# Two INNER feed-forward down projections regrouped into sevens over five blocks each

## The chip, the cores and the metric

The program runs on one core of one Trainium2 chip. Its engines work side by side: TensorE (PE) multiplies matrices, VectorE (DVE), ScalarE (ACT) and GpSimd (POOL) compute element by element, and SyncE (SP) issues transfers (DMA), as POOL also does. Each engine works through its own instructions in program order and waits on semaphores for the others. The metric is the device time of one execution in microseconds (us); lower is better.

## The reference

The kernel computes two layers of a decoder on x of 512 tokens by 1024 features, all in fp32. Each layer is a feed-forward network (FFN), a mix of attention and convolution, and a second FFN:

```
def rms_norm(x, gain):
    inv = lax.rsqrt(jnp.mean(x * x, axis=-1, keepdims=True) + NORM_EPS)
    return (x * inv) * gain

def swiglu(h, w_gate, w_up, w_down):
    return (jax.nn.silu(h @ w_gate) * (h @ w_up)) @ w_down

for l in range(2):
    x = x + 0.5 * swiglu(rms_norm(x, ffn1_norm[l]), ffn1_wg[l], ffn1_wu[l], ffn1_wd[l])
    h = rms_norm(x, mix_norm[l])
    z = h @ w_in[l]                      # q, k, v and three convolution streams
    attn_out = sliding_window_attention(q, k, v, attn_sink[l])
    conv_out = short_conv(b_gate, c_gate, h_conv, conv_w[l])
    x = x + jnp.concatenate([attn_out, conv_out], axis=-1) @ w_out[l]
    x = x + 0.5 * swiglu(rms_norm(x, ffn2_norm[l]), ffn2_wg[l], ffn2_wu[l], ffn2_wd[l])
return rms_norm(x, final_norm)
```

The FFN's inner width is 2816. The change touches the product with `w_down` in two of the four FFNs.

## The kernel before

**Products.** An fp32 product is made of three matmuls. Every operand is kept as a high part (`wh`, or the first of a pair) and a low part (`wl`, what the cast to the high part lost), and hi x hi, lo x hi and hi x lo are added up in PSUM. A weight tile of 128 partitions by 1024 values (two row blocks of 128 by 512 columns) is loaded by SP into a buffer `raw` (`load`, L205), cast by ACT into `wh` (L221) and subtracted by DVE into `wl` (L222). There are eight `raw` buffers (`stock`) and four each of `wh` and `wl`. The input side of a product, a "form", is made in the same way: `fb11`, `fb21`, `fb22`, `ft1` to `ft4`.

**Blocks and sevens.** The inner width is cut into 11 blocks of 256. A table per FFN lists its stages. `FIRST` is the first FFN of layer 0, `INNER` the second FFN of layer 0 and the first of layer 1, `LAST` the last. A stage "w" computes gate and up for two blocks, "p" one block plainly. "s" is the down projection of four blocks by the Strassen-Winograd scheme: instead of eight products of quarter matrices it makes seven, from sums of quarters. "d" is the plain down projection of the blocks listed. INNER does the blocks 1 to 4 and 5 to 8 by sevens and 9 and 10 plainly, by `down_end`.

**Sums of weights.** The seven products of an "s" need five weight quarters or sums: a11, s1 (two quarters), a12, s3 (two quarters) and a22, each as two `raw` tiles (halves h = 0 and 1). The sums with two quarters come from a load by SP and an accumulating transfer by POOL onto the same tile (L216). The further sums are made on the chip: s2 = a11 + s1 by DVE in place in a11's tile (L249), s4 = a12 + s2 by a POOL transfer that adds one `raw` tile onto another (`raw<-raw`, L277). A buffer is free for a later load when its last reader, which may be such a transfer, is done. The order of the products is a11, a12, s2, s3, s1, a22, s4 (`FORMS`); in the program of before PE writes them to accumulators x, w, x, y, x, y, x. `share` walks through them and calls `stream` for each weight tile: 12 matmuls of 128x512. After a product, DVE adds the accumulator to x (L1005).

**Activations on their way.** A "w" stage leaves its gated values in planes of 16-bit halves (`pl`, ACT L1227), which SP transposes by DMA (`send`, L1233, into `pt`) and ACT copies into `raw_a` (`join`, L1287). The pair of blocks that is computed last before the sevens is 9 and 10; its accumulators are worked on while the first group of sevens runs.

**What sets the order.** The program is written as one sequence. `need_raw` issues loads a number of units ahead (`LOAD_AHEAD`), `need_split` makes casts and subtractions ahead of use (`SPLIT_AHEAD`), and `tc.issue_after(x)` puts an instruction behind another in the order; a scheduler then places the rest. On an engine, and on SP's and POOL's queues, the order is fixed: what is behind a waiting instruction waits too. In `send` the transposes of a pair stand behind the latest weight load that had been issued.

One form per group, `fb22`, is made "far": ACT writes its negative into the low part and casts the high part, and a POOL transfer adds the original to the low part (`split_far`, L227 to L229), so that DVE has no part in it.

Of the kernel before, what the change touches and what calls it, by code (L numbers as in the profile page):

```python
# [16 lines left out]
P = 128  # L17
# [17 lines left out]
    ("s", 2), ("d", (10,)), ("s", 6),  # L35
)
INNER = (
    ("p", 0), ("w", 1), ("d", (0,)), ("w", 3), ("w", 5), ("w", 7), ("w", 9), ("s", 1), ("s", 5),
    ("d", (9, 10)),
)  # L40
LAST = INNER[:-1] + (("d", (9, 10)),)
# [28 lines left out]
    ((1, 1, -1), (0, 1, 1)), ((0, 1, 1),),  # L70
)
# [4 lines left out]
def trunk_kernel(  # L76
# [130 lines left out]
    def need_raw(u):  # L207

        while state["raw"] <= min(u, len(units) - 1):
            n = state["raw"]  # L210
            _, _, kc, _, wide = units[n][0]
            r = stock(f"raw_{n}", shape=(P, kc, wide * (2 if n in beside else 1)))
            if n >= OPEN:
                load(r, n, 0, kc)
            for more in () if n in beside else units[n][1:]:
                nc.gpsimd.dma_start(out=r, in_=rows_of(*more), accum_op=ALU.add)  # L216
            raw_of[n] = r
            state["raw"] += 1
# [12 lines left out]
    def need_split(g):  # L231
        while state["split"] <= min(g, len(order) - 1):
# [3 lines left out]
            if what in (None, "wide", "room", "far"):  # L236
                need_raw(u if far else u + LOAD_AHEAD)
                raw = raw_of.pop(u)
            elif isinstance(what, tuple):

                what, h, how = what
                far = how == "far"
# [21 lines left out]
            if what == "room":  # L264
                hi, lo = both(f"wx_{n}", shape=(P, 2, 2, S))
            else:
                hi = wpool.tile(shape, F32R, tag="wh", bufs=4, name=f"wh_{n}")
                lo = wpool.tile(shape, F32R, tag="wl", bufs=4, name=f"wl_{n}")
# [4 lines left out]
            if isinstance(order[n][1], tuple):  # L273
# [13 lines left out]
                for i in done:  # L287
                    del raw_of[u + 2 * i + h]
            split_of[n] = (hi, lo)
            state["split"] += 1  # L290
            if far:

                with tc.issue_after(sent.ins):
                    need_raw(u + LOAD_AHEAD + (4 + h if isinstance(order[n][1], tuple) else 0))
# [110 lines left out]
    def down_end(acts, blocks, norm, open_):  # L405

        a, b = blocks
        held = []

        def tile_of(n):  # L410
            while len(held) <= n:
                held.append(take_split(min(SPLIT_AHEAD, 4 - len(held)))[1:])
            return held[n]

        def products(acc, t, n):
            tok = slice(t * P, (t + 1) * P)
            fresh = (t, n // 2) not in open_
            ah, al = acts[blocks[n % 2]]
            wh, wl = tile_of(n)
            for k in range(2):  # L420
                for i, (x_, w) in enumerate(((ah, wh), (al, wh), (ah, wl))):
                    nc.tensor.matmul(
                        acc,
                        x_[:, k, tok],
                        w[:, k, :],
                        start=n % 2 + k + i == 0 and fresh,
                        stop=n % 2 == 1 and k == 1 and i == 2,
                        skip_group_check=not fresh,
                    )

        def bank(t, o):
            if (t, o) in open_:
                return open_[t, o]
            return psum("mm", [P, S], f"down_{state['group']}_{t}_{o}")

        by_hand()
        for t in range(2):
            for o in range(2):
                acc = bank(t, o)
                for i in range(2):  # L440
                    products(acc, t, 2 * o + i)
                yield t, o, acc
        ahead = state["group"]
        for o in range(2):
            accs = {t: bank(t, o) for t in (2, 3)}
            for i in range(2):
                n = 2 * o + i
                for t in (2, 3):
                    products(accs[t], t, n)
                    if i:  # L450
                        yield t, o, accs[t]
                if n in (1, 2):
                    norm.pull()
                if n:
                    need_split(ahead + n)

    def plan():
# [15 lines left out]
        def seven(at, how):  # L473


            u = len(units)
            for what in (((0, 0),), ((1, 0), (1, 1)), ((0, 1),), ((1, 0), (0, 0)), ((1, 1),)):
                for h in range(2):
                    add_unit(*(at(o, j, h) for o, j in what))
            forms = EARLY if how == "early" else FORMS  # L480
            order.extend((u, (what, h, how)) for what in forms for h in range(2))

        def ffn(wg, wu, wd, stages):
            for what, b in stages:
# [13 lines left out]
                if what == "s":  # L498
                    seven(
                        lambda o, j, h: (wd, 2 * b + KC // 2 * j + 2 * h, 2, o * S, S),  # L500
                        "early" if (what, b) == stages[-1] else "share",
                    )
# [3 lines left out]
                for half in range(2):  # L506
                    for k in b:
                        u = add_unit((wd, 2 * k, 2, half * S, S))
                        if half == 0 or not end or stages is not LAST:
                            room = end and stages is not LAST and (half, k) == (0, b[0])  # L510
                            order.append((u, "room" if room else "wide"))
# [227 lines left out]
    class Seven:  # L739
# [3 lines left out]
        def __init__(self, full, room, name, far=()):  # L743
            self.full, self.room, self.name, self.forms, self.sums = full, room, name, {}, None
            self.far = far

        def make(self, *names):
            for what in names:
                if what in self.forms:
                    continue  # L750
                hi, lo = both(f"f{what}_{self.name}")
                self.forms[what] = (hi, lo)
                b11, b12, b21, b22 = (
                    self.full[j][:, :, t * H : (t + 1) * H] for j in range(2) for t in range(2)
                )
                if what in ("t2", "t3") and not self.sums:
                    self.sums = self.room(self.name)
                    nc.vector.tensor_sub(self.sums[0], b12, b22)
                if what == "t2":
                    nc.vector.tensor_sub(self.sums[1], self.sums[0], b11)  # L760
                if what == "t1":
                    nc.vector.tensor_sub(b12, b11, b12)
                if what == "t4":
                    nc.vector.tensor_add(self.sums[1], self.sums[1], b21)
                src = {"b11": b11, "b21": b21, "b22": b22, "t1": b12}.get(what)
                if src is None:
                    src = self.sums[0 if what == "t3" else 1]
                (split_far if what in self.far else split)(hi, lo, src)

# [185 lines left out]
    def stream(accs, wh, wl, xh, xl, h, start, norm=None):  # L955

        for u in range(2):
            tok = slice(u * P, (u + 1) * P)
            for k in range(2):
                for i, (x_, w) in enumerate(((xh, wh), (xl, wh), (xh, wl))):  # L960
                    nc.tensor.matmul(  # L961
                        accs[u],
                        x_[:, 2 * h + k, tok],
                        w[:, k, :],
                        start=start and h + k + i == 0,
                        stop=h + k == 2 and i == 2,
# [5 lines left out]
    def share(  # L972
# [6 lines left out]
        for step, (acc, operand, start) in enumerate(chains):  # L979
# [3 lines left out]
            xh, xl = ops.forms[operand]  # L983
# [5 lines left out]
            for h in range(2):  # L989
# [824 lines left out]
```

## Time and profile before

| | us |
|---|---|
| runs | 1638.86, 1637.8, 1638.81 (median 1638.81) |
| profiled execution | 1635.43 |
| its span on the core | 1633.7 |
| PE busy | 1624.8 (99%) |
| DVE busy | 1304.0 (80%) |
| ACT busy | 1142.0 (70%) |
| first INNER sevens and plain down, PE | 721.20 to 820.90 |
| second INNER sevens and plain down, PE | 1045.90 to 1146.00 |

In the profile's rows, names stand without their buffer numbers (`wl<-raw,wh` is any such subtraction), L numbers are lines of the kernel before, SPq and POOLq are the queues from which transfers are issued, and "to landing" is the time from issue until the data has arrived. A row of waits gives the engine and line that waited, what it waited for, the total, the number of times and the longest. A row of an engine in order of time gives the start, the duration, the instruction and, in brackets, how long the engine had been idle before it and what ended that.

### The profile page before, as it was taken

What the parts mean: (1) busy time and instruction counts of PE and PEld (TensorE: products, weight loads), DVE (VectorE), ACT (ScalarE), POOL (GpSimd) and SP (SyncE); (2) the same over time, 40 slices, a digit from 0 to 9 for tenths busy, and PEclk for the clock granted to TensorE, in tenths of its full rate; (3) what the DMA queues carried; (4) which work ended last, traced back from release to release, by engine and by line L of the source; (5) the groups of instructions that cost most, each with busy time, mean ns of one, the idle gap of its engine ahead of it and who ended that gap; (6) DMA issues with size and microseconds to landing.
All of it is one profiled execution on the core that took longest, in us unless ns stands there. A gap on an engine that the chain in (4) does not pass through costs nothing.

```text
span 1633.7 us, 21063 instructions
## 1 busy us (share of the span) xinstructions
PE 1624.8 (99%) x7544; PEld 1353.7 (83%) x7544; DVE 1304.0 (80%) x1718; ACT 1142.0 (70%) x1597; POOL 192.1 (12%) x172
## 2 busy tenths in 40 slices
PE   9999999999999999999999999999999999999998
PEld 7888888898888888888888888888988888888886
DVE  7987779878899867789688667887678987778885
ACT  7457777558867677786476777865597775777864
POOL 0011111100120111112001111110002101111111
PEclk9999999999999999999999999999999999999999
DMA  9379999934685788999737888997147857899992
GB/s 258 88 196 220 222 224 251 219 90 88 177 200 129 206 207 218 210 235 254 217 82 202 211 211 220 234 246 199 45 108 196 202 132 196 215 213 234 222 248 84
DMA packets 295292, 310.74 MB, mean 190 GB/s; under 512 B 116980, under 2 KB 179476, under 8 KB 295188
## 3 DMA queue, kind: packets, MB, share of 16 engines
q1 hardware_dynamic: 252660, 230.09, 48.7%
q0 software_dynamic: 41824, 78.65, 28.3%
q8 instruction: 59, 0.97, 0.2%
q10 hardware_dynamic: 704, 0.66, 0.1%
q14 instruction: 45, 0.37, 0.1%
HBM read 263.74 MB, written 2.10 MB: 163 GB/s over the span
## 4 chain that ended last, share of the span: by engine, by line
PE 93%; ACT 5%; DVE 1%; DMA 1%; issue 1%; SPq 0%; ACTq 0%; DVEq 0%
PE x L961 25%; PE y L961 13%; PE x_s L961 10%; PE w L961 6%; PE y_s L961 5%; PE up L1118 4%; PE down L383 3%; PE w_s L961 3%; PE acc L313 3%; PE acc L314 3%; PE acc L316 2%; PE acc L360 2%; PE x_m L961 1%; PE xt L705 1%; PE y_m L961 1%; ACT p L1589 1%
## 5 line engine op out<-in xcount | busy, mean ns | idle before, releaser
L222 DVE TENSOR_TENSOR wl<-raw,wh 128x1024 fp32r<-128x1024 f32 (+1 forms) x493 | 599.2, 1221 | 211.3 <-ACT wh L221 204.8
L221 ACT CAST wh<-raw 128x1024 fp32r<-128x1024 f32 (+1 forms) x493 | 511.7, 1044 | 300.3 <-PE y L961 37.5
L961 PE MATMUL x<-wh,ft 128*128 128x512 f32 x608 | 187.2, 389 | 0.0
L961 PE MATMUL y<-wh,ft 128*128 128x512 f32 x608 | 187.1, 389 | 0.0
L961 PE MATMUL x<-wh,fb 128*128 128x512 f32 x608 | 187.1, 389 | 0.0
L961 PEld LDWEIGHTS x<-wh,ft 128*128 128x128 f32 x608 | 114.2, 188 | 23.7
L961 PEld LDWEIGHTS x<-wh,fb 128*128 128x128 f32 x608 | 114.2, 188 | 23.7
L961 PEld LDWEIGHTS y<-wh,ft 128*128 128x128 f32 x608 | 114.1, 188 | 23.7
L961 PE MATMUL x<-wl,fb 128*128 128x512 f32 x304 | 118.3, 389 | 0.0
L961 PE MATMUL x<-wl,ft 128*128 128x512 f32 x304 | 118.3, 389 | 0.0
L961 PE MATMUL y<-wl,ft 128*128 128x512 f32 x304 | 118.3, 389 | 0.0
L1287 ACT COPY raw_a<-pt 128x1024 uint16<-128x1024 uint16 x76 | 103.3, 1360 | 17.9 <-DMA pt<-pl 17.8
L216 POOL DMA_DIRECT2D raw<-in_ffn_wu_dram x39 | 47.0, 1208 | 546.3 <-DMA raw<-in_ffn_wu_dram 351.4
L313 PE MATMUL acc<-hh,wh 128*128 128x512 f32 x240 | 94.0, 392 | 0.0
L961 PE MATMUL w<-wh,fb 128*128 128x512 f32 x304 | 93.6, 389 | 0.0
L314 PE MATMUL acc<-hl,wh 128*128 128x512 f32 x240 | 93.5, 390 | 0.0
L316 PE MATMUL acc<-hh,wl 128*128 128x512 f32 x240 | 93.4, 389 | 0.0
L961 PE MATMUL y_s<-wh,ft_s 128*128 128x512 f32 x256 | 78.8, 389 | 0.0
L961 PE MATMUL x_s<-wh,ft_s 128*128 128x512 f32 x256 | 78.8, 389 | 0.0
L249 DVE TENSOR_TENSOR raw<-raw,raw 128x1024 f32<-128x1024 f32 x58 | 70.5, 1219 | 9.1 <-DMA raw<-in_ffn_wd_dram 6.0
L216 POOL DMA_DIRECT2D raw<-in_ffn_wg_dram x39 | 46.8, 1206 | 235.2 <-DMA raw<-in_ffn_wu_dram 88.4
L961 PE MATMUL x_s<-wh,fb_s 128*128 128x512 f32 x240 | 74.0, 389 | 0.2 <-DVE x L1005 0.2
(370 smaller groups left out, 3431.7 us busy)
## 6 DMA issues: line engine op xcount, KB each, us to landing
raw<-in_ffn_wu_dram SPq DMA_DIRECT2D x120, 512.0 KB, 5.1
raw<-in_ffn_wd_dram SPq DMA_DIRECT2D x104, 512.0 KB, 6.9
raw<-in_ffn_wg_dram SPq DMA_DIRECT2D x80, 512.0 KB, 5.4
raw<-in_ffn_wu_dram POOLq DMA_DIRECT2D x39, 512.0 KB, 8.4
raw<-in_ffn_wg_dram POOLq DMA_DIRECT2D x39, 512.0 KB, 5.9
raw<-in_w_in_dram SPq DMA_DIRECT2D x36, 512.0 KB, 4.5
raw<-in_ffn_wd_dram POOLq DMA_DIRECT2D x32, 512.0 KB, 8.6
raw<-raw POOLq DMA_DIRECT2D x20, 512.0 KB, 8.9
```

The source lines that it names most:

```text
L216: nc.gpsimd.dma_start(out=r, in_=rows_of(*more), accum_op=ALU.add)
L221: cast = nc.scalar.copy(hi, raw)
L222: state["sub"] = eng.tensor_sub(lo, raw, f32(hi))
L249: nc.vector.tensor_add(a11, a11, s1)
L313: nc.tensor.matmul(acc, hi[:, k, :], rhs[k][0], start=k == first, stop=False)
L314: nc.tensor.matmul(acc, hi[:, k, :], rhs[k][1], start=False, stop=False)
L316: state["product"] = nc.tensor.matmul(acc, lo[:, k, :], rhs[k][0], start=False, stop=k == last)
L360: nc.tensor.matmul(accs[j][:, t * H : (t + 1) * H], w[:, k, :], x_, start=t + k + i == 0, stop=k == KC - 1 and i == 2, skip_group_check=True,)
L383: nc.tensor.matmul(acc, a[:, k, tok], w[:, k, :], start=i + k + n == 0 and fresh[t], stop=i == last and k == 1 and n == 2, skip_group_chec ...
L961: nc.tensor.matmul(accs[u], x_[:, 2 * h + k, tok], w[:, k, :], start=start and h + k + i == 0, stop=h + k == 2 and i == 2, skip_group_chec ...
L1118: nc.tensor.matmul(accs[t], x_[:, tok], w[:, k, :], start=j + k + i == 0, stop=j == 3 and k == 1 and i == 2,)
L1287: nc.scalar.copy(room.rearrange("p c (n z) -> p c z n", z=2)[:, :, z, :], turned[0][:, NT * z + 2 * c : NT * z + 2 * c + 2, :],)
```

## The change

INNER's blocks 1 to 10 are now done by two groups of seven products over five blocks each: the first group takes blocks 1 to 4 and, as a fifth, block 5; the second takes 7 to 10 and block 6. The fifth block is split into quarters of half the height: its two row blocks of 128 play the parts of the two halves of the group's inner dimension. So each of the seven products gets, beside its two full weight tiles (128x1024), a third of half the size (128x512, h = 2), and each form gets an extra form of 128x256 (`fx...`, with `sx` for its sums). The plain down projection of blocks 9 and 10 and `down_end` are gone. The half weight tiles and extra forms lie in a pool of 11 smaller buffers (`g2`) that also holds other small tiles.

The order in which the 15 `raw` tiles of a group are loaded is given by `THREES` (or `THREES_EARLY` for the last group of a stage): the number of each tile of a11, s1, a12, s3 and a22. In `THREES`, s1's half tile is loaded as number 7 and s3's as number 13, behind the full tiles of a22 (11 and 12). Loads are issued two units further ahead (`LOAD_AHEAD + 2`). The transposes of the last pair are ordered behind the load that was the latest at step 5 of its products (`seen`), and not behind the latest when they are written; its copies into `raw_a` come from tick 12 on. In the INNER groups the forms `fb11` and `ft1` are made far, as `fb22`. FIRST and LAST keep sevens of four blocks, in another notation.

```diff
 INNER = (
-    ("p", 0), ("w", 1), ("d", (0,)), ("w", 3), ("w", 5), ("w", 7), ("w", 9), ("s", 1), ("s", 5),
-    ("d", (9, 10)),
+    ("p", 0), ("w", 1), ("d", (0,)), ("w", 3), ("w", 5), ("w", 7), ("w", 9), ("s", (1, 3, 5)),
+    ("s", (7, 9, 6)),
 )
-LAST = INNER[:-1] + (("d", (9, 10)),)
+LAST = INNER[:-2] + (("s", (1, 3, None)), ("s", (5, 7, None)), ("d", (9, 10)))
...
+PAIRS = ((0, 1), (2, 3), (4, 5), (6, 7), (8, 9))
+THREES = ((0, 1, 2), (3, 4, 7), (5, 6, 9), (8, 10, 13), (11, 12, 14))
+THREES_EARLY = ((0, 1, 2), (3, 4, 10), (5, 6, 8), (7, 9, 11), (12, 13, 14))
+EXTRA = (("b21+",), ("t1", "t2+"), ("b22", "t4", "t3+"), ("t1+", "t4+"), ("b22+",), (), ())
...
-            r = stock(f"raw_{n}", shape=(P, kc, wide * (2 if n in beside else 1)))
+            room = g2 if kc == 1 else stock
+            r = room(f"raw_{n}", shape=(P, kc, wide * (2 if n in beside else 1)))
             if n >= OPEN:
-                load(r, n, 0, kc)
+                with behind(state["load"] if kc == 1 else None):
+                    load(r, n, 0, kc)
...
-                last = {"a11": 0, "a12": 4, "s2": 2, "s3": 6, "s1": 2, "a22": 8, "s4": 4}[what]
-                need_raw(u + h if far else u + max(last, 4) + h + LOAD_AHEAD)
-                a11, s1, a12, s3, a22 = (raw_of.get(u + 2 * i + h) for i in range(5))
+                last = {"a11": 0, "a12": 2, "s2": 1, "s3": 3, "s1": 1, "a22": 4, "s4": 2}[what]
+                if at is PAIRS:
+                    need_raw(u + max(at[last][h], at[2][h]) + LOAD_AHEAD)
+                else:
+                    need_raw(u + at[last][h] + LOAD_AHEAD + 2)
+                a11, s1, a12, s3, a22 = (raw_of.get(u + at[i][h]) for i in range(5))
...
-            for k in range(2):
+            for k in range(wide):
                 for i, (x_, w) in enumerate(((xh, wh), (xl, wh), (xh, wl))):
...
-                with tc.issue_after(state["load"].ins):
+                with tc.issue_after((seen[0] if wide else state["load"]).ins):
                     nc.sync.dma_start_transpose(
...
+                if step == 5:
+                    seen.append(state["load"])
...
-            plan += [(6 + 2 * gap + gap * n, join, n) for n in range(4)]
+            plan += [(start + gap * n, join, n) for n in range(4)]
...
-            return Seven([raw_act(b), raw_act(b + 2)], room_form, f"s_{whole}_{b}", far=("b22",))
+            far = ("b22",) if x_ is None else ("b11", "t1", "b22")
+            return Seven(full, room_form, f"s_{whole}_{lo}", far=far, extra=extra)
```

Three places in the program, all at the first INNER sevens (layer 0); the second INNER FFN has the same order with other numbers. Here names carry their buffer's number, and the line numbers of the rows marked as after are those of the changed kernel.

SP's queue as PE passes from the last "w" pair to the sevens, before. raw_167 and raw_168 (loaded just ahead) are a12, raw_169 and raw_170 are s3's first load, raw_171 and raw_172 are a22, the DMA_TRANSPOSE rows are the last pair's:

```order
L205 DMA raw_169_6323<-in_ffn2_wd_dram 128x2x512
L205 DMA raw_170_6326<-in_ffn2_wd_dram 128x2x512
L609 DMA gain_3_0_6993<-in_ffn1_norm_dram 128x512
L609 DMA gain_3_1_6994<-in_ffn1_norm_dram 128x512
L205 DMA raw_171_6329<-in_ffn2_wd_dram 128x2x512
L205 DMA raw_172_6363<-in_ffn2_wd_dram 128x2x512
L1233 DMA_TRANSPOSE pt_1_9_6430<-pl_1_9_0_6349 128x8x128
L1233 DMA_TRANSPOSE pt_1_9_6430<-pl_1_9_1_6354 128x8x128
L1233 DMA_TRANSPOSE pt_1_9_6430<-pl_1_9_2_6400 128x8x128
L205 DMA raw_173_6472<-in_ffn2_wd_dram 128x2x512
```

The same place after. raw_171 and raw_173 are s3's full tiles, raw_170 s1's half tile, raw_172 a12's, raw_174 and raw_175 a22's full tiles, raw_176 s3's half tile:

```order
L212 DMA raw_171_6380<-in_ffn2_wd_dram 128x2x512
L212 DMA raw_173_6419<-in_ffn2_wd_dram 128x2x512
L1224 DMA_TRANSPOSE pt_1_9_6440<-pl_1_9_0_6344 128x8x128
L212 DMA raw_170_6361<-in_ffn2_wd_dram 128x512
L1224 DMA_TRANSPOSE pt_1_9_6440<-pl_1_9_1_6349 128x8x128
L1224 DMA_TRANSPOSE pt_1_9_6440<-pl_1_9_2_6402 128x8x128
L212 DMA raw_172_6417<-in_ffn2_wd_dram 128x512
L1224 DMA_TRANSPOSE pt_1_9_6440<-pl_1_9_3_6408 128x8x128
L212 DMA raw_174_6422<-in_ffn2_wd_dram 128x2x512
L212 DMA raw_175_6442<-in_ffn2_wd_dram 128x2x512
L212 DMA raw_176_6461<-in_ffn2_wd_dram 128x512
```

The transposes now stand ahead of a22's two full tiles; s1's half tile stands behind the first transpose, and s3's half tile behind a22's full tiles. raw_174 and raw_175 take the buffers of raw_163 and raw_164 (a11), which are free once the transfers raw_168<-raw_163 and raw_169<-raw_164 have landed.

POOL's queue there, after:

```order
L225 DMA raw_173_6419<-in_ffn2_wd_dram 128x2x512
L225 DMA raw_170_6361<-in_ffn2_wd_dram 128x512
L238 DMA ft1_s_1_1_6532<-raw_a_1_1_5325 128x4x256
L285 DMA raw_168_6322<-raw_163_6149 128x1024
L285 DMA raw_169_6324<-raw_164_6175 128x1024
L238 DMA fb22_s_1_1_6600<-raw_a_1_3_5635 128x4x256
L285 DMA raw_172_6417<-raw_165_6232 128x512
L238 DMA fb11_s_1_7_6716<-raw_a_1_7_6254 128x4x256
L225 DMA raw_176_6461<-in_ffn2_wd_dram 128x512
```

Before, the tile-to-tile transfers were followed by `fb22`'s alone and then by accumulations of the next group; now a half tile's accumulation stands ahead of them and three far forms, a half tile-to-tile transfer and another half tile's accumulation among and behind them.

DVE's order at the second product, a12 (wl_216 to wl_218), after:

```order
L231 TENSOR_TENSOR wl_216_6425<-raw_168_6322,wh_216_6424 128x1024
L1269 TENSOR_TENSOR p7_1_9_1_6252<-p7_1_9_1_6252,gate_1_9_3_6405 128x512
L260 TENSOR_TENSOR raw_165_6232<-raw_165_6232,raw_170_6361 128x512
L231 TENSOR_TENSOR wl_217_6445<-raw_169_6324,wh_217_6444 128x1024
L992 SCALAR_TENSOR_TENSOR x0_89<-x_s_1_1_0_6415,x0_89 128x512
```

The sum onto raw_165 (s2's half tile) stands directly ahead of wl_217, which it had no counterpart for before; the transfer raw_169<-raw_164 waits for wl_217, because it overwrites the tile that wl_217 reads.

DVE's order at the fourth product, s3, after, where wl_224 is its half tile and fxt3 its extra form:

```order
L231 TENSOR_TENSOR wl_224_6588<-raw_176_6461,wh_224_6587 128x512
L747 TENSOR_TENSOR sx_s_1_1_6538<-sx_s_1_1_6538,raw_a_1_5_5945 128x256
L992 SCALAR_TENSOR_TENSOR x2_91<-x_s_1_1_0_6415,x2_91 128x512
L992 SCALAR_TENSOR_TENSOR x2_91<-x_s_1_1_1_6416,x2_91 128x512
L231 TENSOR_TENSOR wl_225_6614<-raw_166_6260,wh_225_6613 128x1024
L231 TENSOR_TENSOR fxt3_s_1_1_6608<-sx_s_1_1_6538,fxt3_s_1_1_6608 128x256
```

Four operations stand between wl_224 and fxt3; PE's matmuls of this half tile need both, and ACT's casts for them in the same order.

More of the change, by code (lines that the diff above doesn't have):

```diff
@@ L509, in ffn @@
                         if half == 0 or not end or stages is not LAST:
-                            room = end and stages is not LAST and (half, k) == (0, b[0])
-                            order.append((u, "room" if room else "wide"))
+                            order.append((u, "wide"))
         for l in range(DEPTH):
@@ L1212, in winograd2 @@
             then = stages[at + 1][0]
+            wide = then == "s" and stages[at + 1][1][2] is not None
+            seen = []
             def apart(t):
```

183 lines of the change are left out of this document (87 added, 96 removed).

## The prediction

> **What bounds the kernel now.** I read the totals and the chain first, then TensorE's waits, then the stage that the change rewrites. From the page:
>
> ```profile
> PE 1624.8 (99%) x7544; PEld 1353.7 (83%) x7544; DVE 1304.0 (80%) x1718; ACT 1142.0 (70%) x1597; POOL 192.1 (12%) x172
> PE 93%; ACT 5%; DVE 1%; DMA 1%; issue 1%; SPq 0%; ACTq 0%; DVEq 0%
> ```
>
> TensorE (PE) is busy 99% of the span and is 93% of the chain that ended last. All that it ever waits for in the trace:
>
> ```profile
> PE idle L150 <- DVE warm L805: 1.2, 1, 1.2
> PE xt L824 <- DMA x<-in_x_dram: 0.3, 1, 0.3
> PE x_s L961 <- DVE x L1005: 0.2, 1, 0.2
> PE y_m L961 <- ACT wh L221: 0.2, 1, 0.2
> ```
>
> Under 2 us in the whole program. So fewer matmuls shorten the span by their own time, and each new wait of PE lengthens it by its own length. Nothing else counts. Now the chain and the stretches (busy time and count of each engine, granted clock, DMA share, GB/s) at the first INNER down projection by sevens, which begins on PE at 721.20; the last row is the second one, in layer 1:
>
> ```profile
> 721.20 5.44 PE x_s L961 x24
> ...
> 737.52 5.44 PE y_s L961 x24
> ...
> 721.20:759.30 38.10, 38.10 (x169) 31.55 (x169) 34.14 (x37) 29.20 (x33) 7.40 (x8) 1.00 1.03 251
> 759.30:797.40 38.10, 38.10 (x169) 31.54 (x169) 33.36 (x34) 22.33 (x23) 4.92 (x5) 1.00 1.03 263
> 721.20:820.90 99.70, 99.70 (x449) 82.73 (x449) 80.91 (x92) 63.83 (x79) 14.72 (x14) 1.00 0.91 225
> 1045.90:1146.00 100.10, 99.91 (x450) 82.61 (x449) 82.45 (x94) 62.46 (x78) 13.28 (x12) 1.00 0.88 216
> ```
>
> 24 matmuls of 128x512 take 5.44 us, 0.2267 each at full clock. PE has no gap, but the DMA share is 1.03 (a share of packet time, so queued packets can carry it past one): in this stage transfers are the tight resource, and the change alters them.
>
> **The change, part by part.** *Matmuls.* Before, an INNER FFN's blocks 1 to 10 take 28 weight tiles of 12 matmuls (two groups of seven products, two tiles each) and 4 plain ones of 24: 432. After, two groups with 14 full tiles of 12 and 7 half tiles of 6 each: 420. So 12 matmuls fewer: 12 x 0.2267 = 2.72 us per FFN, 5.44 in all. FIRST, LAST and the mix stages keep their instructions. This is the only gain on PE.
>
> *The order of loads.* Each half tile brings its own load, and for sums of two weight tiles an accumulating POOL transfer. What such things take, and how they stand in the queues today (SP's waits from 705 to 745, then SP, POOL and ACT in order of time):
>
> ```profile
> SPq L205 <- DMA raw<-raw: 14.1, 2, 11.9
> ...
> 732.78 2.92 SPq L205 DMA_DIRECT2D raw<-in_ffn_wd_dram  x2
> 735.76 7.39 SPq L1233 DMA_TRANSPOSE pt<-pl  x3
> 743.81 1.24 SPq L1233 DMA_TRANSPOSE pt<-pl  x1
> ...
> 720.25 2.41 POOL L216 DMA_DIRECT2D raw<-in_ffn_wd_dram  x2 [10.00 <-DVE wl L222]
> 723.05 0.89 POOL L277 DMA_DIRECT2D raw<-raw  x1 [0.39 <-ACT wh L221]
> ...
> 719.25 2.17 ACT L1227 COPY pl<-u 128x512 uint16<-128x512 uint16 x4
> ```
>
> The loads at 732.78 stood 11.9 us for an accumulation between weight tiles to land and free a buffer, and the transposes behind them in SP's order went out at 735.76, though their first source planes were copied from 719.25 on. The change moves the first transpose ahead of such loads, which costs SP (7.39 + 1.24) / 4 = 2.16 us ahead of whatever follows it. Landings, issue to data (min/median/max), of the SP weight loads and POOL accumulations from 705 to 760, of tile-to-tile accumulations, and of a 256 KB load:
>
> ```profile
> L205 SPq DMA_DIRECT2D raw<-in_ffn_wd_dram x13: 367/419/1017, 707.2 to 752.1; - x13
> ...
> DMA to landing us min/median/max: 4.2/7.7/9.6
> ...
> L216 POOL DMA_DIRECT2D raw<-in_ffn_wd_dram x7: 1188/1197/1231, 707.7 to 758.8; - x7
> ...
> DMA to landing us min/median/max: 7.5/8.7/10.4
> ...
> L277 POOL DMA_DIRECT2D raw<-raw x4: 861/874/886, 723.1 to 766.5; - x4
> ...
> DMA to landing us min/median/max: 8.1/8.9/9.7
> ...
> gain<-in_ffn_norm_dram SPq DMA_DIRECT2D x2, 256.0 KB, 4.2
> ...
> q0 software_dynamic: 835, 2.10, 67.3%
> ```
>
> The last row is POOL's queue from 719 to 736: 2.10 MB used 67.3% of 16 engines for 17 us, 5.45 us per MB. And the vector work in the chains below:
>
> ```profile
> L222 DVE TENSOR_TENSOR wl<-raw,wh 128x1024 fp32r<-128x1024 f32 x43 | 52.3, 1220 | 8.5 <-ACT wh L221 8.3
> ...
> L1005 DVE SCALAR_TENSOR_TENSOR x<-x_s,x 128x512 f32<-128x512 f32 x14 | 9.1, 683 | 0.0
> ...
> L1227 ACT COPY pl<-p 128x512 uint16<-128x512 uint16 x8 | 4.6, 617 | 1.1 <-DVE p L1276 1.1
> ```
>
> PE's own timetable: a product now has two full tiles and a half one, 30 matmuls, 6.80 us. Starting at 721.20, the second product's second tile (wl_217) begins at 730.72 and its low part is wanted at 731.2; the fourth product's half tile (raw_176, wl_224) begins at 747.0, with the low part of its operand fxt3 wanted at 747.3.
>
> *First wait, at wl_217.* On DVE this subtraction stands behind the sum raw_165 += raw_170, so behind raw_170's load and accumulation, and raw_170's load now stands on SP behind the first transpose. Two of the four plane copies are done at about 720.3; transpose 2.16, so 722.5; a 256 KB load, 4.2, so 726.7; POOL starts 0.4 later (0.39 in its row). The trace has no 256 KB accumulation. Bounds: half of the shortest 512 KB one, 3.75, and the median whole, 8.7. I take 6.25, the shortest less its bytes' share (0.25 MB x 5.45 = 1.4, rounded to 1.25), because fixed latency dominates rows of 7.5 to 10.4. So 733.35; the sum 0.69 (as a 128x512 operation), wl_217 1.22: 735.3. PE wants it at 731.2: **a wait of 4.1**, with ends 1.6 and 8.
>
> *Second wait, at wl_224.* raw_169 += raw_164 on POOL is released by wl_217: 735.3 + 0.4, landing 8.9 later, 744.6. Only then is raw_164's buffer free for raw_175, and SP issues raw_176 behind raw_175: 745.0. Load 4.2, POOL 0.4, accumulation 6.25: 755.85. Then wh_224's cast (0.62) and, in DVE's order ahead of what PE needs, wl_224 (0.69), a 128x256 sum (0.42, from the line through 1.22 and 0.69), two additions to x (1.28), wl_225 (1.22) and fxt3 (0.42): 760.5. PE, late by 4.1, arrives at 751.4: **a wait of 9.1**. Without the first wait both sides move together and it stays 9.1. Ends: 5.8 with accumulations of 3.75 and 8.1, and 14 with the load at 7.7 and the others at 8.7 and 9.7. What is late next: the sums behind these loads keep their distance to PE, since PE has slipped by 13 us in front of them.
>
> *More far forms* (a form whose low part is made by an ACT copy and an accumulating POOL transfer instead of a DVE subtraction): three per group where there was one. The one of before makes PE wait nowhere in the rows above. The new ones are made a product ahead, 6.80 us, against a landing of 7 to 9: 0 to 2 us each group. I take 0, as the one of before hid.
>
> *The stage's end.* The two plain blocks, after which the next norm followed, give way to a final group of seven that the norm follows directly. FIRST already ends so, and the list of PE's waits has nothing for it: 0, with 0 to 1 as bounds. DVE's 56 and ACT's 52 more instructions, mostly half and quarter size, are beside PE: DVE was at 34.14 of 38.10 us, so it has about 4 us left per such stretch. The gain vectors' loads, now later on SP, are not wanted before that end.
>
> *Sum per FFN:* -2.72 + 4.1 + 9.1 = +10.5; two of them, **+21.0**. The profiled execution took 1635.43 us (span 1633.7 and 1.7 around it), 3.4 below the median of 1638.81; it would become 1656.4. The same difference on the median gives **1659.8**.
>
> A rule that speaks against these terms: the Trainium skill, page "DMA: Bandwidth & Descriptors", section "Anatomy of one DMA — SWDGE (gpsimd) path", gives a transfer issued by GpSimd about 2.0 us of fixed time plus bytes at 436 GB/s, so by an estimate from that page 2.6 us for 256 KB and 3.2 for 512 KB. By it the chain would be short, raw_176 would be ready at about 747, both waits would be below 1 us, and the change would save some 4 us. The trace disagrees here: 7.5 to 10.4 us for 512 KB, in queues that were full.
>
> **The rivals.** *Hidden, so faster.* Transfers land early enough, and only the 12 matmuls show: -5.4, or -3 with a fraction of a us left over, 1633 to 1636. This decides if raw_176's accumulation has landed by 747.3 - 0.6 - 4.0 = 742.7, 13 us ahead of my sum. For it: the transposes no longer queue, and an emptier queue makes landings short (4.2 is the shortest). Against: raw_175 cannot be issued before the tile-to-tile accumulation lands, and the same kind of hold is the 11.9 in SP's row. Accumulations of about 3 us on all three links would do it.
>
> *Only one wait.* The first vanishes because raw_170 lands in time, or the second is half as long: -2.72 + 3 to 8 per FFN, +1 to +11 in all, 1640 to 1650.
>
> *DMA becomes the bound.* POOL's queue carries per FFN four more 512 KB far forms and six more 256 KB accumulations, 3.5 MB, 19 us of all 16 engines at 5.45 per MB. The stage had 0.91 x 99.7 = 91; 110 over 97 us is 1.13, where 1.03 was the most that PE rode out. The 0.10 x 97 = 10 us beyond come in part while PE waits anyway; if none does, each FFN costs 20 and the time is 1679.
>
> **How the numbers follow.** Both waits as worked out, +11 to +32: 0.60, and 1659.8 is its middle. One wait, +4 to +11: 0.16; a small remainder, within 0.2% (3.3 us, about what a measurement of this kernel can tell from no change): 0.03. Hidden, faster by more than that: 0.11. DMA-bound or longer waits, above +32: 0.10. The range runs from +2 to +37, 1641 to 1676: it leaves out the hidden case and the top of the last one. Slower 0.86, same 0.03, faster 0.11.
>
> **What would show it.** In the changed profile PE's waits should list, in both INNER groups, a wait at w_s (the second product) of 2 to 8 us released by DVE wl, and one of 6 to 14 at y_s released by DVE (the fxt3 form) or ACT. The chain should pass through raw<-raw, SP loads and accumulations near 735 to 760. The far forms are right at 0 if no wait ends on an fb_s or ft_s transfer. PE's busy time should fall by 5.4. I am wrong if PE's waits stay below 2 us, or if 256 KB accumulations land in about 3; if waits spread evenly over all seven products, DMA or DVE throughput is the bound and not these two places.

## The result: 1704.62 us, 4% slower, and the profile after

The changed kernel takes 1704.62 us (median of 4 runs, 1696.84 to 1708.84) against 1638.3 us before (4 runs, 1637.49 to 1638.86): a ratio of 1.04, 95% interval 1.0359 to 1.0441. The direction was forecast; the size was not. The loss is 66.3 us where 21.0 were worked out, and the time lies above the range. The profiled execution took 1707.12 us, its span is 1705.3.

From the page of the kernel after, the totals:

```profile
PE 1638.4 (96%) x7520; PEld 1357.8 (80%) x7520; DVE 1315.7 (77%) x1774; ACT 1161.3 (68%) x1649; POOL 213.2 (13%) x192
```

PE has 24 matmuls fewer and is yet busy 13.6 us longer than before (1624.8). The second view, PE's waits after (engine, line, what it waited for; total us, times, longest), shows the rest:

```profile
PE w_s L943 <- DVE wl L231: 25.7, 3, 13.4
PE y_s L943 <- ACT fxt_s L230: 18.1, 2, 10.0
PE x_s L943 <- ACT wh L230: 9.8, 2, 6.6
PE y_s L943 <- DVE fxt_s L231: 3.4, 2, 1.7
```

These four rows are the waits in the two INNER FFNs, 57.0 us where there were 0.2. All of them lie in the first group of seven of each FFN; the second groups have none. The span grew by 1705.3 - 1633.7 = 71.6 us: 57.0 of waits, 13.6 of PE's busy time and about 1 elsewhere. The busy time should have fallen by 5.4, so its matmuls became 13.6 + 5.4 = 19.0 us slower. Two stretches of the first group (busy time and count of each engine, granted clock, DMA share, GB/s) and matmul rows behind its longest wait show why:

```profile
722.90:732.50 9.60, 9.60 (x44) 7.84 (x43) 7.70 (x10) 9.16 (x15) 5.08 (x5) 1.00 0.92 190
745.00:749.50 4.50, 4.40 (x10) 3.14 (x10) 1.23 (x3) 0.00 (x0) 2.18 (x2) 0.55 1.55 142
```

```profile
745.09 0.80 PE L943 MATMUL w_s<-wl,fb_s 128*128 128x512 f32 x1 [12.01 <-DVE wl L231]
745.68 1.05 PE L943 MATMUL w_s<-wh,fb_s 128*128 128x512 f32 x2
746.53 0.63 PE L943 MATMUL w_s<-wl,fb_s 128*128 128x512 f32 x1
...
748.24 1.01 PE L943 MATMUL w_s<-wh,fb_s 128*128 128x512 f32 x2
```

Three matmuls start every 1.28 us behind the wait (745.68, 746.96, 748.24), 0.427 each, instead of 0.2267, and the granted clock of that stretch is 0.55. Where nothing interrupts them it takes some 14 matmuls until the full rate is back. There are six waits of more than 3 us, three in each FFN, so in this kernel a stop costs 19.0 / 6, about 3 us on average, beside the wait itself.

Where the transfers went shows in the DMA view of the first group after, from 724 to 757 (issues with their size and median time from issue to landing):

```profile
raw<-in_ffn_wd_dram POOLq DMA_DIRECT2D x2, 512.0 KB, 10.9
raw<-raw POOLq DMA_DIRECT2D x2, 512.0 KB, 19.4
raw<-in_ffn_wd_dram SPq DMA_DIRECT2D x2, 256.0 KB, 20.0
ft_s<-raw_a POOLq DMA_DIRECT2D x1, 512.0 KB, 18.7
fb_s<-raw_a POOLq DMA_DIRECT2D x1, 512.0 KB, 21.8
raw<-in_ffn_wd_dram POOLq DMA_DIRECT2D x1, 256.0 KB, 13.3
raw<-raw POOLq DMA_DIRECT2D x1, 256.0 KB, 13.7
pt<-pl SPq DMA_TRANSPOSE x4, 13.4
```

and SP's queue there in order of time:

```profile
724.51 1.24 SPq L1224 DMA_TRANSPOSE pt<-pl  x1
725.80 0.57 SPq L212 DMA_DIRECT2D raw<-in_ffn_wd_dram  x1
726.46 7.80 SPq L1224 DMA_TRANSPOSE pt<-pl  x2
734.35 0.72 SPq L212 DMA_DIRECT2D raw<-in_ffn_wd_dram  x1
735.16 10.68 SPq L1224 DMA_TRANSPOSE pt<-pl  x1
```

s1's half tile, issued at 725.80, was on the chip by 729.8, when its accumulation on POOL began; that took 13.3 us, to 743.2: PE's 12.0 at w_s. a12's half tile is a plain load, issued at 734.35 behind three transposes; it landed 20.0 us later: PE's 6.6 at x_s. Then raw_169 += raw_164 took 18.2 us where before it took 9.6, and raw_176 came behind it as foreseen: PE's 8.2 + 1.7 at y_s.

### The profile page after: what moved, and what is told of

Same layout as the page of the kernel before. It is cut to its first block, busy times and chain, and to the rows that moved or that the text cites. A ratio compares the mean times of both kernels' runs of the same rounds, so it can differ in the third digit from the quotient of the medians.

```text
span 1705.3 us, 21220 instructions
## 1 busy us (share of the span) xinstructions
PE 1638.4 (96%) x7520; PEld 1357.8 (80%) x7520; DVE 1315.7 (77%) x1774; ACT 1161.3 (68%) x1649; POOL 213.2 (13%) x192
## 4 chain that ended last, share of the span: by engine, by line
PE 46%; DMA 3%; ACT 3%; DVE 1%; issue 1%; SPq 0%; ACTq 0%; DVEq 0%; POOLq 0%
PE x L943 12%; PE x_s L943 7%; PE y L943 6%; PE y_s L943 4%; PE w L943 3%; DMA raw<-in_ffn_wd_dram 3%; PE up L1107 3%; PE w_s L943 1%; PE down L391 1%; PE acc L368 1%; PE acc L321 1%; PE acc L322 1%; PE acc L324 1%; PE z_s L943 1%; ACT wh L230 1%
## 5 line engine op out<-in xcount | busy, mean ns | idle before, releaser
L231 DVE TENSOR_TENSOR wl<-raw,wh 128x1024 fp32r<-128x1024 f32 (+2 forms) x515 | 611.8, 1194 | 263.8 <-ACT wh L230 257.0
L230 ACT CAST wh<-raw 128x1024 fp32r<-128x1024 f32 (+2 forms) x515 | 521.9, 1020 | 366.3 <-DMA raw<-in_ffn_wd_dram 70.3
L1280 ACT COPY raw_a<-pt 128x1024 uint16<-128x1024 uint16 x76 | 103.2, 1358 | 17.5 <-DMA pt<-pl 17.5
L260 DVE TENSOR_TENSOR raw<-raw,raw 128x1024 f32<-128x1024 f32 (+1 forms) x62 | 73.4, 1187 | 32.6 <-DMA raw<-in_ffn_wd_dram 29.6
L943 PE MATMUL x_s<-wh,ft_s 128*128 128x512 f32 x256 | 85.7, 418 | 9.8 <-ACT wh L230 9.8
L225 POOL DMA_DIRECT2D raw<-in_ffn_wd_dram x40 | 45.5, 1201 | 252.6 <-DMA raw<-in_ffn_wd_dram 112.4
```

The costliest lines, as they stand in the source:

```text
L230: cast = nc.scalar.copy(hi, raw)
L231: state["sub"] = eng.tensor_sub(lo, raw, f32(hi))
L260: nc.vector.tensor_add(a11, a11, s1)
L943: nc.tensor.matmul(accs[u], x_[:, k if h == 2 else 2 * h + k, tok], w[:, k, :], start=start and h + k + i == 0, stop=h == last and k == wi ...
L1280: nc.scalar.copy(room.rearrange("p c (n z) -> p c z n", z=2)[:, :, z, :], turned[0][:, NT * z + 2 * c : NT * z + 2 * c + 2, :],)
```

## The experiments

The theory that the result suggested, A: the last pair's transposes, now issued between POOL's accumulations and half tile loads, slow those and themselves, and the half tiles behind them come late. Its rival, B: POOL simply has too many transfers (three far forms, half accumulations), wherever the transposes stand. A third cause, s3's half tile behind a22's full tiles, was in the forecast. Before's time is from runs on the same chip each time, 1636.1 to 1637.9.

**late**: the transposes go back behind the latest load.

```diff
-                with tc.issue_after((seen[0] if wide else state["load"]).ins):
+                with tc.issue_after(state["load"].ins):
```

> One part undone: the last pair's transposes stand behind the latest load again, so s1's and a12's half tiles are issued ahead of all four. Theory A (the transposes, issued between POOL's accumulations, slow those and themselves from some 7 to 13 us and more, and with them the first two waits of 12 and 7 us in each INNER group): the waits at w_s and x_s fall below 2 us each, the wait at the half tile of s3 (10 us) stays, the clock dips less; PE waits about 20 us in all, time 1655 to 1670. Theory B (too many POOL transfers for the queue, wherever the transposes stand): the accumulation of s1's half tile still takes over 11 us, PE waits over 40 us, time 1685 to 1705.

Measured: 1673.37 us, 31 below the change. PE's largest waits in this run:

```profile
PE y_s L943 <- ACT fxt_s L230: 21.0, 2, 10.8
PE x_s L943 <- DVE wl L231: 3.1, 2, 1.5
```

The waits at w_s are gone, those at x_s are 7.3 in both FFNs together (3.1 and two of 2.1), and the wait for s3's half tile stays, 10.8 of it in the first FFN. That is the picture of theory A, but with 30 us of waits and not 20, and the time is 3 us above its range. s1's accumulation landed 8.9 us after its issue.

**far1**: only b22 is far.

```diff
-            far = ("b22",) if x_ is None else ("b11", "t1", "b22")
+            far = ("b22",)
```

> One part undone: in the INNER groups only b22 is made by a POOL transfer; b11 and t1 are split by DVE as before. Theory A (transposes among accumulations): the accumulation of s1's half tile still lands late, since four accumulations and three transposes stay beside each other; waits at w_s 8 to 12 and x_s 3 to 7 us remain, time 1685 to 1705. Theory B (number of POOL transfers): that accumulation lands in 6 to 9 us, PE's waits fall to some 25 us in all, time 1655 to 1675.

Measured: 1670.0 us. PE's waits:

```profile
PE x_s L943 <- ACT wh L230: 23.4, 2, 16.0
PE y_s L943 <- ACT fxt_s L230: 4.7, 2, 4.5
```

s1's accumulation landed in 6.5 us though the transposes still stood around it, and PE waited 29.9 us in all. Here theory B had the right number, against A. But what stays is the wait at x_s for a12's half tile, which stands behind three transposes. So each of the two, taken away alone, removes about half of the loss. The shares do not add up: the three single edits that follow take away 24 to 39 us each, and all five together would be more than twice the loss. Two reasons show below: a wait can hide another that comes behind it, and the same transfers slow each other.

**plain**: the transposes become plain copies at the same place; the turning is left out.

```diff
-                    nc.sync.dma_start_transpose(
-                        turned[0][:, :, t * P : (t + 1) * P],
-                        planes[t].rearrange("p z n -> p (z n)"),
+                    nc.sync.dma_start(
+                        out=turned[0][:, :, t * P : (t + 1) * P],
+                        in_=planes[t].rearrange("p z (a n) -> p (z a) n", n=P),
```

> In the last pair of each INNER FFN the four transposes are replaced by plain copies of the same 256 KB at the same place in SP's queue, so the planes arrive untransposed: the turning is left out, everything else is computed. Theory A in its narrow form (it is the transposing, by small packets, that slows the accumulations beside it): the copies land in 4 to 8 us, s1's accumulation in 6 to 9, PE's waits fall to 20 to 30 us, time 1655 to 1675. Theory B, or A in its wide form (any transfer of that size there does it): waits stay over 45 us, time 1690 to 1705.

Measured: 1680.8 us, between the two. PE's waits, and the landings from 724 to 757 as above:

```profile
PE x_s L943 <- ACT wh L230: 33.5, 2, 16.8
PE y_s L943 <- ACT fxt_s L230: 3.5, 1, 3.5
```

```profile
pt<-pl SPq DMA_DIRECT2D x4, 256.0 KB, 14.0
...
raw<-raw POOLq DMA_DIRECT2D x2, 512.0 KB, 11.6
...
raw<-in_ffn_wd_dram POOLq DMA_DIRECT2D x1, 256.0 KB, 8.4
```

By kind, POOL's accumulations land in a median of 8.4 to 13.5 us instead of 10.9 to 21.8 (all kinds of that stretch but one, a 256 KB one between tiles, issued behind the wait: 3.5 for 13.7), so the turning itself harms them. The copies and the half tile behind them are as late in this run as the transposes were (14.0 for 13.4; a12's half tile 19.6 for 20.0), turned or not. The narrow form of A accounts for the first wait, which is gone (0.2 at w_s), and not for the one at x_s.

**s1first**: s1's half tile is loaded as number 5.

```diff
-THREES = ((0, 1, 2), (3, 4, 7), (5, 6, 9), (8, 10, 13), (11, 12, 14))
+THREES = ((0, 1, 2), (3, 4, 5), (6, 7, 9), (8, 10, 13), (11, 12, 14))
```

> One size in the order of loads: s1's half tile becomes number 5 of its group (before a12's tiles and before the transposes) instead of 7. If the first wait comes from its load and accumulation standing behind the first transpose and beside the others, the wait at w_s (12 us) falls below 3 and the time by 20 to 30 us, to 1675 to 1685, with the wait for a12's half tile (behind three transposes) still there. If the accumulation is slow wherever it stands, or if the two waits only change places, less than 8 us are gained: 1697 to 1705.

Measured: 1675.48 us, 29 below the change, with this wait and 6.0 us of smaller ones:

```profile
PE x_s L943 <- ACT wh L230: 27.3, 2, 15.9
```

The wait at w_s is gone, as the first reading said, and part of it came back at x_s (27.3 for 9.8), for the half tile behind the transposes. That tile, issued at 731.3, took 18.0 us and landed at 749.3 (at 754.4 in the change); PE, which reached it at 749.5 in the change, now comes at 735.2 and waits there instead.

**s3first**: s3's half tile ahead of a22's full tiles.

```diff
-THREES = ((0, 1, 2), (3, 4, 7), (5, 6, 9), (8, 10, 13), (11, 12, 14))
+THREES = ((0, 1, 2), (3, 4, 7), (5, 6, 9), (8, 10, 11), (12, 13, 14))
```

> One size in the order of loads: s3's half tile becomes number 11 of its group, ahead of a22's two full tiles, instead of 13 behind them; transposes and far forms stay as in the change. If the wait at the fourth product comes from that load standing behind raw_175, which waits for a tile-to-tile transfer to land, then the waits at y_s (18.1 + 3.4 us in both FFNs) fall below 6 and the time by 15 to 22 us, to 1682 to 1690; the waits at w_s and x_s stay. If the wait is the general lateness of the queue, y_s keeps more than 12 us and the time stays above 1697.

Measured: 1666.05 us, 39 below the change, more than either reading allowed.

```profile
PE w_s L943 <- DVE wl L231: 21.2, 2, 13.6
PE x_s L943 <- ACT wh L230: 1.5, 1, 1.5
```

No wait at y_s is left: the second wait was that one place in the queue. The waits at w_s stay. Those at x_s nearly vanish because a12's half tile, issued at 733.18, landed after 16.9 us, at 750.1, when PE, held for 13.6 us at w_s, had only just come to it. Why it landed 3 us faster than in the change is open.

**late_s3**: late and s3first together, three far forms kept. **late_s3_far1**: the same with far1. **s3_far1**: s3first and far1, transposes early.

> Two parts: transposes behind the latest load (as in the run late) and s3's half tile ahead of a22's tiles; three far forms per group stay. If the two causes named so far (half tiles queued behind transposes, s3's half tile queued behind a22) are all, PE's waits fall below 5 us and the time is 1633 to 1640. If the three far forms by themselves overload POOL's queue, as the run far1 suggests, some product still waits 3 to 10 us per FFN: 1643 to 1660.

> The same two parts, and only b22 far. If the waits are queueing of transfers, none is left above 1 us, PE's busy time is about 1619.4 and the time 5 us below the kernel before: 1631 to 1634. If DVE, which takes back two subtractions of 1.22 us per group, then becomes late, PE waits on DVE for 1 to 3 us per group and the time is 1636 to 1645.

> Transposes early as in the change, but s3's half tile ahead of a22's and only b22 far. If the early transposes do harm by themselves, the wait for a12's half tile, issued behind three of them, stays at 5 to 16 us per FFN as in the run far1: 1652 to 1668. If it took the far forms beside them, PE's waits fall below 6 us in all: 1634 to 1642.

Measured: late_s3 1657.14 us (ratio 1.0125, 1.0112 to 1.0138), 15.4 us of PE waits, none above 3.4: three far forms do cost, as its second reading said. late_s3_far1 1648.96 us (1.0071, 1.0054 to 1.0088), above both of its readings, with waits of 11.8 us spread over several places. s3_far1 1659.45 us, its first reading, with one wait in each FFN. PE's largest waits of late_s3_far1, then of s3_far1:

```profile
PE x_s L943 <- DVE wl L231: 5.2, 2, 2.7
PE w_s L943 <- ACT fxb_s L230: 3.0, 2, 1.8
```

```profile
PE x_s L943 <- ACT wh L230: 22.5, 2, 16.5
```

With all but the transposes' place in common, the early transposes cost 10.5 us (1659.45 - 1648.96) and put the whole wait on the half tile behind them.

**late_s1_s3_far1**: late_s3_far1 with s1's half tile as number 5, that is `THREES = ((0, 1, 2), (3, 4, 5), (6, 7, 9), (8, 10, 11), (12, 13, 14))`. **late_s1_s3_far1_b21**: besides, `b21+` is made in step 6 of the last pair and not after the first product.

> As late_s3_far1, and s1's half tile as number 5 of its group. In late_s3_far1 DVE stands 5.1 us before the sum onto s2's half tile, for that tile's accumulation, and PE then waits 2.5 to 2.7 us at x_s. If that is the cause, the waits at x_s fall below 1 us per FFN, those for the extra form at w_s (4.0 in all) and at y_s stay or shrink, and the time is 1638 to 1644. If DVE's work is simply too much for the stage, waits of the same sum appear elsewhere: 1646 to 1652.

> The same, and the extra form of b21 is made at the end of the last pair's products instead of after the first product of the sevens. If the waits at w_s come from that form being placed late behind the casts and subtractions of the third product, they vanish too; PE's waits in the INNER groups are then below 3 us in all, PE's busy time 1620 to 1623, the time 1632 to 1637, at or just below the kernel before. If a saturated DVE or DMA is the limit, the waits move to later products and the time stays above 1642.

Measured: 1638.49 us (ratio 1.0017, 1.0005 to 1.0028), in the range of its first reading, with 6.5 us of waits: the one for the sum onto s2's half tile fell from 5.2 to 0.9, as that reading said, but a new one stands at x_s. And 1644.19 us (1.0047, 1.0023 to 1.0071), a miss for its first reading; the time is that of the second, but the largest wait is for one buffer and not spread. Waits of the first, then of the second:

```profile
PE x_s L943 <- ACT fxt_s L230: 4.9, 2, 2.7
```

```profile
PE x_s L943 <- ACT fxt_s L230: 6.8, 1, 6.8
```

The wait is for the extra form of t2. In the program it takes a `g2` buffer that is free when a transfer has landed: by the trace's releasers, in the first kernel the first transpose, which reads its source plane from that buffer (it landed 8.0 us after its issue at 735.66; the form's cast began at 743.72), in the second a tile-to-tile accumulation. So transposes behind the loads are not free either: their planes hold the buffers that the extra forms need. The next run puts that to the test.

**first_turn_early** and **two_turns_early**: late_s1_s3_far1 with the first one, or the first two, of the four transposes early.

```diff
-                with tc.issue_after(state["load"].ins):
+                with tc.issue_after((seen[0] if wide and t < 2 else state["load"]).ins):
```

(`not t` in place of `t < 2` for the first.)

> As late_s1_s3_far1, but the first of the four transposes is ordered early, as in the change; the other three stay behind the latest load. In late_s1_s3_far1 the extra form of t2 waited for the buffer of that transpose's source plane until it had landed (743.4), and PE waited 2.2 and 2.7 us for the form at x_s. If one early transpose frees the buffer without crowding the accumulations, these waits vanish, PE waits below 2 us in the INNER groups, PE's busy time is about 1620 and the time 1632 to 1635, some 0.2% below the kernel before. If already one transpose among the accumulations delays them, PE waits 3 to 10 us per FFN at w_s or x_s and the time is 1642 to 1655.

> The same with the first two transposes early. If the harm of the early transposes grows with their number beside the accumulations, the second one (which landed 13 us after its issue in the change) brings waits of 2 to 8 us per FFN for a12's and s3's half tiles behind it: 1638 to 1652. If only the far forms made them harmful, there is no wait and the time is that of the run with one early transpose, within 2 us.

Measured: 1636.62 us (1.0001, 0.999 to 1.0013) and 1635.28 us (0.9993, 0.998 to 1.0006), against 1636.43. Neither can be told from the kernel before. With one, the wait for t2's extra form went, as expected, and one for b21's came (4.5 us at w_s in the profiled execution, which was the slowest of the twelve). The second transpose did no harm: the times are within 2 us of each other, as the second reading of two_turns_early said. That does not make the far forms alone the cause: in s3_far1, with one far form, four early transposes cost 10.5 us. All four with s1's half tile in front and one far form were not run, so it is open whether the number of early transposes counts or which tile stands behind them. In the profiled execution of two_turns_early PE waits 3.5 us in the groups and is busy 1622.1, not 1619.4; that eats the 5.4 us of matmuls.

**before_early**: the early transposes alone, in the kernel before.

```diff
-                with tc.issue_after(state["load"].ins):
+                with tc.issue_after((seen[0] if then == "s" and stages is INNER else state["load"]).ins):
...
+                if step == 5:
+                    seen.append(state["load"])
```

> One part of the change alone, in the kernel before: the last pair's transposes of each INNER FFN stand behind the load seen at step 5 of its products, so three of them stand ahead of a22's two full tiles, with full tiles, four-block groups and one far form as before. If transposes beside POOL's accumulations slow both by themselves, the accumulations of s3 and a12 (7.5 to 10.4 us before) and the transposes (3.2 to 5.7 us before) land in 11 to 20 us, and PE waits 3 to 12 us per FFN: 1644 to 1665. If it takes the half tiles and the additional far forms too, landings grow by some us only, which the slack of full tiles covers: 1635 to 1640.

Measured: 1642.02 us (ratio 1.004, 1.0021 to 1.0059). Landings at the second INNER sevens, from 1045 to 1075, in the kernel before and then in this one:

```profile
raw<-raw POOLq DMA_DIRECT2D x2, 512.0 KB, 9.6
gain<-in_mix_norm_dram SPq DMA_DIRECT2D x2, 256.0 KB, 3.9
fb_s<-raw_a POOLq DMA_DIRECT2D x1, 512.0 KB, 7.8
pt<-pl SPq DMA_TRANSPOSE x4, 5.6
```

```profile
raw<-raw POOLq DMA_DIRECT2D x2, 512.0 KB, 18.9
fb_s<-raw_a POOLq DMA_DIRECT2D x1, 512.0 KB, 20.7
gain<-in_mix_norm_dram SPq DMA_DIRECT2D x2, 256.0 KB, 14.8
pt<-pl SPq DMA_TRANSPOSE x4, 20.2
```

and at the first INNER sevens, from 718 to 748, in this kernel (before: 9.6, 4.2, 7.4 and 4.7):

```profile
raw<-raw POOLq DMA_DIRECT2D x2, 512.0 KB, 12.5
gain<-in_ffn_norm_dram SPq DMA_DIRECT2D x2, 256.0 KB, 15.1
fb_s<-raw_a POOLq DMA_DIRECT2D x1, 512.0 KB, 14.2
pt<-pl SPq DMA_TRANSPOSE x4, 7.7
```

At the second place the same transfers take two to four times as long, with nothing new in the queues; at the first, accumulations and transposes take 1.3 to 1.9 times as long, and only the small plain load behind the transposes over three times. That is the first reading on landings at the one place and in part at the other; why the two differ is open. PE's waits in the groups are only 5.1 us; that the full tiles behind these landings have more time in hand would explain it, but was not followed in the trace. On the cost it lies between the readings.

## Why the prediction was wrong

The span came out 50.6 us above the 21.0 forecast: 17.5 from the waits at w_s, 9.8 from a wait that was not in the sum, 3.3 from those at y_s, 19.0 from slower matmuls and about 1 elsewhere.

*The gain of 5.44 us* holds: the page counts 24 matmuls fewer, and at full clock they start every 0.2267 us as before.

*First wait, 4.1 with ends 1.6 and 8*: it was 12.0 and 13.4. The place was right (wl_217 behind the sum that waits for raw_170's accumulation). The step that failed is the price of that accumulation, "I take 6.25": it took 13.3. The transposes were counted as 2.16 us of SP's time ahead of raw_170, and not as transfers that would now run beside POOL's accumulations. The rows used for every landing came from a stretch in which the transposes ran later, beside one far form. Alone (before_early) the early transposes take accumulations between tiles from 9.6 to 12.5 in the first INNER FFN and to 18.9 in the second; with one far form (far1) raw_170's took 6.5, with late transposes 8.9. It took both parts of the change to reach 13.3. The upper ends were also added up wrongly: 8.7 for the accumulation gives a wait of 6.6 and not 8, and the values named for the second wait give 15.9 and not 14.

*A wait that was not in the sum*: 6.6 and 3.2 us at x_s for a12's half tile. The order showed it behind the first three transposes; it needs no accumulation before its product, and I had not followed its load at all. It landed 20.0 us after issue. Without the wait at w_s in front of it, it is as long as that one was (15.9 and 11.4 in s1first).

*Second wait, 9.1*: 8.2 + 1.7 = 9.9 and 10.0 + 1.7 = 11.7, for the cause given; s3first takes it away by one number. Here the estimate of 6.25 for the half accumulation met 6.5 (that of raw_176, issued at 773.1). That the wait came out so near is luck all the same: the chain took about 14 us longer than worked out (18.2 for 8.9 between the tiles, 8.5 for 4.2 for raw_176's load), and PE came to it about 12 us later, for the wait at x_s and the slow matmuls behind the waits.

*Far forms, taken at 0*: no wait ends on one, but they are not free. late_s3 to late_s3_far1, 8.2 us, is what two of them per group cost with the transposes late, and in the change itself, with the transposes early, 34.6 (far1).

*The clock, not in the sum*: 19.0 us, the largest term that was missing. Each wait was priced at its own length, with PE at full rate behind it. The Trainium skill, page "TensorE: Matmul & The Clock Gate", section "What's actually happening", says that the array's clock is halved after an idle window of about 3.4 us and restored after a busy one. The trace agrees on the rate (0.427 for 0.2267 a matmul); it stays low for about 6 us of matmuls (756.1 to 762.6 behind the 6.6 us wait), longer than one such window. On the length of the idle time it does not agree: in late_s3_far1 2.67 us were enough,

```profile
737.23 0.80 PE L943 MATMUL x_s<-wl,ft_s 128*128 128x512 f32 x1 [2.67 <-DVE wl L231]
737.82 1.05 PE L943 MATMUL x_s<-wh,ft_s 128*128 128x512 f32 x2
...
739.10 1.05 PE L943 MATMUL x_s<-wh,ft_s 128*128 128x512 f32 x2
```

again three matmuls in 1.28 us, while in late_s1_s3_far1 a wait of 2.21 us was followed by the full rate. That is at least part of why late_s3_far1, with no wait above 2.7, has PE busy for 1628.6 us where 1619.4 were expected.

*The stage's end*: 0, right. *The rule that spoke for a gain* (the Trainium skill, page "DMA: Bandwidth & Descriptors", section "Anatomy of one DMA — SWDGE (gpsimd) path", weighed in the prediction): in the changed kernel's first group the accumulations take 6.5 to 21.8 us, none near its 2.6 or 3.2; one of 256 KB in the run plain, issued behind the long wait, took 3.5. *DMA as the bound*: the nearest of the rivals in size (1679), and its sign was there, a DMA share of 1.55 behind the first wait. But the loss is not spread over the products; the waits sit at three half tiles.

What stays open: why transposes and accumulations slow each other so much. That the turning matters is shown (plain), and that plain copies beside POOL's transfers are late as well; what causes it inside the transfers is not. In the first INNER FFN of the unchanged kernel the same move did less harm than in the second, and no run says why.

## What to carry to other kernels

A landing time holds only for the transfers that ran beside it. When a transfer is moved in a queue, ask what is in flight where it arrives, and price both again; a kind that has never run beside another there has no row. A wait of TensorE can cost more than its length: here six waits of 3.2 to 13.4 us cost some 3 us each on average on top, in matmuls at about half rate; one of 2.67 did the same and one of 2.21 did not, and no limit was measured. Waits of one chain do not add up: with one taken away, the next can grow. And follow every small tile that is added, also those that need no sum: the one behind a queue sets the time.

## What was not expected of the hardware

A 128x512 load took 4.2 us before (the gain's) and 20.0 beside transposes and accumulations; with nothing but the transposes moved the gain's took 15.1, and an accumulation between tiles 12.5 to 18.9 us for 9.6. Issuing shows it too: the last transpose holds SP for 10.68 us, where the four of before took 1.24 to 3.63.
